# A two-layer decoder trunk on one core: every on-chip array placed at a multiple of 64 bytes

## The chip, the cores and the metric

The program runs on one core of one Trainium2 chip, in one launch. The metric is the device time of that launch in microseconds (us), the median of several executions. A core has TensorE for matrix products (its rows in a profile are PE, and PEld for the loading of the stationary operand), VectorE (DVE), ScalarE (ACT), GpSimd (POOL) and SyncE (SP), which here only issues DMA transfers. On-chip memory for operands has 128 partitions; an array takes the same byte range in each partition, so an array's place is one byte address.

## What is computed

The reference runs 256 tokens of width 2048 through two layers, all in float32. Every sub-layer has the same frame (`c` is one vector per sequence; `silu(c) @ ada_w` gives a shift, a scale and a gate per sub-layer):

```python
h = rmsnorm(x, m_pre) * (1.0 + sc_m) + sh_m
x = x + gt_m * rmsnorm(mixer(h), m_post)
h = rmsnorm(x, f_pre) * (1.0 + sc_f) + sh_f
x = x + gt_f * rmsnorm((silu(h @ wg) * (h @ wu)) @ wd, f_post)
```

The mixer of layer 0 is a diagonal state space (S5) beside a gated delta rule, that of layer 1 a gated linear attention (GLA). The feed-forward part has 5632 hidden features. Nearly all the work lies in products of 256 tokens with weights that are read once from memory, some 600 MB of them.

## The kernel before

**The big products.** A float32 product is made of three products in the format float32r: the weight w is split exactly into wh + wl, the activation h into hh + hl, and `mm3` (L219) adds hh\*wh (L222), hh\*wl (L223) and hl\*wh (L224) into the same PSUM tile. `wload` (L193) fetches a weight tile of 512 KB into `w` (L216, issued by SyncE), and `split` (L144) turns it into `wh` by a copy on ScalarE (L147) and into `wl` by a subtraction on VectorE (L148).

**Two kinds of product.** `gemm_tok` (L226) has tokens on the output's partitions: the activation (128 x 128) is stationary, and 512 columns of `wh` or `wl` are the moving operand. The feed-forward parts, the output projections and the value and gate projections of the mixers are of this kind. `gemm_feat` (L254) has features on the output's partitions: there 128 x 128 of `wh` or `wl` is stationary, and 256 columns of the activation move. A profile row names the moving operand first: `mm<-wh,hhi` moves the weight, `mm<-hhi,wh` moves the activation.

**The storage.** Four pools lie one behind the other in each partition: `cst` (constants), `ring` (six slots for `w`, three for `wh`, three for `wl`, 4096 bytes each), `sm` (small arrays, made by the helper `small`, L72) and `blk` (32 blocks of 4096 bytes, for activations and everything large). The last 12 k-chunks of weights at the ends of an output projection and the starts of the next product are *held*: they are split into blocks of `blk` instead of ring slots (L200 to L201), under the names `hwh` and `hwl`, so that all products of the first 128 tokens can run before those of the second 128. Activations that are operands of the big products (`hhi`, `hlo`, `ahi`, `alo`, `yhi` and so on) always lie in `blk`.

An allocator places the arrays in the order in which their pools were opened, and rounds each array's size up to 32 bytes. Addresses of the built program before:

```
array                     address   remainder by 64   by 128
ident (cst, first)          16512          0              0
sel (cst, 4 bytes)          19072          0              0
vcols (cst, behind sel)     19104         32             32
w  (ring, first slot)       22880         32             96
wh (ring, first slot)       47456         32             96
wl (ring, first slot)       59744         32             96
acc (sm, 4096 bytes)        72032         32             96
first block of blk          96320          0             64
end of blk                 227392
```

All ring slots have the same remainders as the first, since a slot has 4096 bytes, and so have all blocks of `blk`.

**The order of the work.** The weight tiles come in the order in which the products are written. Between them, `tick` (L164) emits steps of other streams: the conditioning (`ada`, L283: one tile of `ada_w` per step, summed by VectorE at L321), S5's tables and scan, and the delta rule's solve. The splits are moved up in the order, so that the next tiles are split while TensorE works on the one before. `wh` and `wl` have three slots each, so ScalarE's copy of a tile waits until TensorE has used up the slot.

Of the kernel before, what the change touches and what calls it, by code (L numbers as in the profile page):

```python
"""Two conditioned decoder layers (S5 + gated DeltaNet + SwiGLU, then GLA + SwiGLU) on one core.

Products with the big weights run as float32r passes over exact splits: w = wh + wl and h = hh + hl,
where each part fits float32r, and hh*wh + hh*wl + hl*wh carries float32's accuracy.
Arrays live on chip as lists of [128, 1024] float32 blocks of one shared pool.
"""
# [6 lines left out]
F32 = mybir.dt.float32  # L13
# [9 lines left out]
P = 128  # L23
# [4 lines left out]
# Order of the program:  # L28
# how far splits of weights move up while the start, the mixer's products and its end are emitted
BOOST = (100, 30, 100)  # L30
# steps of a stream per weight tile: S5's tables, the conditioning by sub-layer, S5's scan, the delta rule's solve
# [4 lines left out]
# streams that VectorE takes up behind the latest split of weights  # L36
BEHIND = ("prep", "solve")
# which of the conditioning's first parts TensorE sums
# [3 lines left out]
class Net:  # L42
# [21 lines left out]
    def pin(s, ins):  # L64
        """Keeps an instruction without operands from taking its storage long before its time."""
        return s.tc.keep_in_program_order(ins)

# [10 lines left out]
    def small(s, shape, dt=F32, tag=None, bufs=2):  # L78
        return s.sm.tile(shape, dt, tag=tag or "s" + "_".join(map(str, shape)), name="small", bufs=bufs)

# [1 line left out]
    def consts(s):  # L82
# [14 lines left out]
        # rows 0, 32, 64 and 96 are one  # L97
        s.sel = s.cst.tile([P, 1], F32, name="sel")
        nc.vector.tensor_reduce(out=s.sel, in_=s.ident[:, 0::32], axis=AX.X, op=ALU.add)

    def picks(s):
        nc = s.nc
        # pick[:, j, 32:64] picks every fourth token from j on, with zeros to both sides
        z = s.b(name="pick0")[:, :384].rearrange("p (j n) -> p j n", j=4)
        nc.gpsimd.memset(z, 0.0)
        for j in range(4):
            nc.gpsimd.tensor_copy(z[:, j, 32:64], s.ident[:, j::4])
        s.pick = s.cst.tile([P, 4, 96], F32R, name="pick")
        nc.scalar.copy(s.pick, z)

# [1 line left out]
    def rsqrt(s, out, x, scale, eps, add=None):  # L112
        """out = (x*scale + eps)^-0.5 for small operands, to float32's accuracy; (x + add)^-0.5 * scale with add."""
        nc = s.nc
        shape = [x.shape[0], int(x.free_size())]
        if shape == [P, 1]:
            # w = -x/2, then y = y * (y * y * w + 1.5), from a seed by the bits of w
# [26 lines left out]
    def split(s, hi, lo, x):  # L144
        """hi + lo = x exactly, both in float32r."""
# [8 lines left out]
    def step(s, name):  # L154
        """Emits one step of a stream; False at its end."""
# [28 lines left out]
    def finish(s, name):  # L184
        while s.step(name):
            pass
# [7 lines left out]
    def wload(s, ap, a, b, hold=False):  # L194
        """A tile of weights [128, a, b] on chip and split: [(hi, lo)] along a."""
# [23 lines left out]
    def mm3(s, ps, lhs, rhs, st, en):  # L219
        """ps (+)= lhs^T rhs over split operands."""  # L220
# [5 lines left out]
    def gemm_tok(s, W, n0, nw, kcs, lhs, ps=None, st=True, en=True, hold=0, late=False):  # L226
        """[256 tokens, nw] = h @ W[:, n0:n0+nw] over k-chunks kcs, one PSUM tile per 128 tokens.
        The last `hold` k-chunks of weights stay on chip for the second 128 tokens, which then run behind
        the first (after all of theirs, if late)."""
# [3 lines left out]
        per = 4  # L233
# [20 lines left out]
    def gemm_feat(s, W, n0, kcs, lhs, nw=256):  # L254
        """[nw features, 256 tokens] = (h @ W[:, n0:n0+nw])^T, one PSUM tile per 128 features."""
# [14 lines left out]
    def vectors(s):  # L270
        """Vectors over features as columns: V[name] is [128, chunks]."""
# [19 lines left out]
    def row_sums(s, ps, wv, k, first, last):  # L291
        """ps[32j + any, :] (+)= silu(c)_k^T W_k for the four k-chunks k + j, side by side in the array's columns."""
# [4 lines left out]
    def ada(s, layer, sec, finish, pe=False):  # L297
        """Generator: one of the six parts of silu(c) @ W + B, by halves; finish(q, sums, e) gets a quarter's partial
        sums, still to be added over the partitions that e selects. The products run on VectorE, or on TensorE."""
# [84 lines left out]
    def squares(s, x, out):  # L384
        """out = the sums of squares of [128, n <= 512] x."""
# [3 lines left out]
    def rstd(s, x, out):  # L389
        """1 / rms of one token tile [128, 2048] in two halves."""  # L390
# [12 lines left out]
    def pre(s, x, t, S, H, hi, lo):  # L403
        """h^T = ((x / rms(x)) * S + H)^T of token tile t, split, into the blocks of k-chunks hi and lo.
        1 / rms goes in with the transposing product (first tile, shortest chain) or before it (least of TensorE)."""
# [39 lines left out]
    def out_part(s, W, kcs, lhs, y):  # L445
        """Adds h @ W over some k-chunks to y, or makes y where there is none."""
# [14 lines left out]
    def post(s, W, kcs, lhs, y, x, G, then, hold):  # L461
        """x + G * rms-normed (y + h @ W), in place of x; then(t) follows for each token tile."""
# [34 lines left out]
    def transposed(s, src, hi, lo, t, deep=None):  # L497
        """Four [128 tokens, 128] pieces of src into a block of k-chunks, split."""
# [45 lines left out]
    def gla(s, h, x, G, then):  # L544
# [3 lines left out]
        # gate logits: low-rank, tokens first, then by features  # L548
# [53 lines left out]
        # q and k by features, scaled by their decays  # L602
# [29 lines left out]
        # attention weights, keys on partitions: [tile 0 own, tile 1 own, tile 0 for queries of tile 1]  # L632
# [28 lines left out]
        # v, and the heads' outputs  # L661
# [31 lines left out]
    def gla_mm(s, ps, f, items):  # L693
        """Products over the two feature chunks of a head: the first chunk's sums are kept on chip by PSUM."""
# [9 lines left out]
    def s5_load(s):  # L704
        """b and c, two groups of a state on the partitions."""
# [9 lines left out]
    def s5_prep(s):  # L715
# [37 lines left out]
        # sin and cos of th, reduced to [-pi, pi]  # L753
# [50 lines left out]
        # columns: state on partitions, tiles along the free axis  # L804
# [17 lines left out]
        # e^(i*4*theta*c), c < 64  # L822
        s.s5_cos = [s.b(name="s5cos") for _ in range(2)]
        s.s5_sin = [s.b(name="s5sin") for _ in range(2)]
        for hf in range(2):
# [10 lines left out]
            while m < 64:  # L836
# [3 lines left out]
                # e^(i*m) from e^(i*m/2), squared  # L840
# [16 lines left out]
        # b and c with the state on partitions: [128, 32 tiles, 16]  # L857
# [24 lines left out]
        # d on the diagonal of the first lag  # L882
# [16 lines left out]
        for ig in range(4):  # L899
# [44 lines left out]
            # lags 0..3 of the groups' kernels  # L944
# [25 lines left out]
    def s5_run(s, pu, out):  # L970
        """Generator: u (PSUM, tokens on partitions, 512 channels a half) to the split y by features, in out."""
# [8 lines left out]
        for hf in range(2):  # L980
            yT, hi, lo = None, None, None
            for qq in range(2):
                ig = hf * 2 + qq
                # chunks of 4 tokens on the partitions, picked by columns of the identity
# [40 lines left out]
                # states before each chunk  # L1025
# [12 lines left out]
                # outputs: [64 chunks, (j, p)] per group  # L1038
# [49 lines left out]
    def gdn_masks(s):  # L1088
        nc = s.nc
        # level l: rows in the lower half of block b of 2^(l+1), columns (b, 2^l)  # L1090
# [9 lines left out]
    def gdn_conv(s, ps, fc, out, cw):  # L1100
        """silu of the causal convolution of one feature chunk [128, 256], out of PSUM."""
# [6 lines left out]
    def gdn_gates(s, ps):  # L1108
        """beta and the running sums of g from the projections a, b (tokens on partitions)."""
# [18 lines left out]
        # softplus(z) = max(z, 0) + log1p(e), the latter with what 1 + e rounds off  # L1128
# [442 lines left out]
```

## Time and profile before

| | us |
|---|---|
| median of three executions | 2604.7 |
| the three executions | 2600.22, 2604.7, 2609.11 |
| span of the profiled execution, first to last instruction | 2602.8 |
| PE busy, share of the span | 2508.7, 96% |
| DVE busy | 1733.1, 67% |
| ACT busy | 1108.0, 43% |

The profile is of one execution, of which it gives the span alone; the span is 1.9 us under the median, and the three executions lie 8.9 us apart. In a row of a group, `xN` is the number of instructions, and behind it stand their busy time together and the mean of one. "Min/median/max" rows give durations in nanoseconds. Products overlap in TensorE, so one lasts longer than the time from its start to the start of the next; what a stretch of products costs is read from starts. PEclk is the clock that was granted to TensorE as a share of the full one. The profile shows these stages: up to 165 us the first conditioning and `u`, to 607 us the mixer of layer 0, 659 to 1403 us its feed-forward part, 1410 to 1829 us GLA, 1865 to 2593 us the last feed-forward part.

### The profile page before, as it was taken

The page shows a single profiled execution, that of the slowest core. Times are in us where ns is not written, and L with a number is a line of the kernel's source. Part 1 is how long each engine was busy: PE and PEld are TensorE (multiplying, and loading weights), DVE is VectorE, ACT ScalarE, POOL GpSimd, SP SyncE. Part 2 cuts the span into 40 slices and gives each one's busy share as a digit, 9 for nine tenths or more (in the row PEclk, how much of TensorE's full clock was granted, in tenths as well). Part 3 has the DMA queues.
Part 4 walks back from the last instruction along what each step waited for, and adds up shares of the span by engine and source line. Part 5 has one row for each costly group of instructions (what it writes and reads, how often), then busy time and mean ns, then how long its engine had stood idle before and what let it go on. Part 6 is the DMA issues. An engine that isn't in the chain of part 4 may idle for free.

```text
span 2602.8 us, 34554 instructions
## 1 busy us (share of the span) xinstructions
PE 2508.7 (96%) x13142; PEld 2028.4 (78%) x13142; DVE 1733.1 (67%) x2294; ACT 1108.0 (43%) x1416; POOL 84.8 (3%) x135
## 2 busy tenths in 40 slices
PE   5999999987999999999998999999999999999998
PEld 2577889865777888887786897787788788888886
DVE  6866797678677676777778677676655544444446
ACT  3354553435334444433445533444544444433443
POOL 1120001000000000000000000000000000000000
PEclk9999999998999999999999999999999999999999
DMA  8877567576788888988886586788466565556554
GB/s 277 318 246 251 171 208 249 179 261 235 237 299 289 293 289 286 314 305 303 292 283 213 159 272 222 244 292 275 150 209 210 190 187 186 181 184 191 184 182 137
DMA packets 298983, 615.15 MB, mean 236 GB/s; under 512 B 24368, under 2 KB 61680, under 8 KB 298816
## 3 DMA queue, kind: packets, MB, share of 16 engines
q1 hardware_dynamic: 294240, 604.32, 70.0%
q0 software_dynamic: 2304, 4.93, 0.6%
q10 hardware_dynamic: 2272, 3.68, 0.4%
q8 instruction: 103, 1.69, 0.3%
q14 instruction: 64, 0.52, 0.1%
HBM read 610.10 MB, written 2.10 MB: 235 GB/s over the span
## 4 chain that ended last, share of the span: by engine, by line
PE 84%; DVE 6%; DMA 5%; ACT 3%; issue 2%; SPq 0%; ACTq 0%; DVEq 0%; POOL 0%
PE mm L223 25%; PE mm L222 24%; PE mm L224 24%; DMA w<-in_ada_w_dram 4%; PE tp L295 2%; DVE wl L148 1%; DVE small L321 1%; PE tp L503 1%; PE tp L331 1%; ACT small L428 1%; DMA w<-in_w_out_dram 1%; ACT small L387 1%; PE tp L1247 1%; PE tp L1253 1%; PE tp L1006 1%
## 5 line engine op out<-in xcount | busy, mean ns | idle before, releaser
L148 DVE TENSOR_TENSOR wl<-w,wh 128x1024 fp32r<-128x1024 f32 x722 | 878.7, 1222 | 559.2 <-ACT wh L147 557.6
L147 ACT CAST wh<-w 128x1024 fp32r<-128x1024 f32 x722 | 755.4, 1047 | 1131.7 <-PE mm L224 960.5
L222 PE MATMUL mm<-wh,hhi 128*128 128x512 f32 x1720 | 685.4, 399 | 7.4 <-DVE hhi L433 4.5
L223 PE MATMUL mm<-wl,hhi 128*128 128x512 f32 x1720 | 684.1, 398 | 6.5 <-DVE wl L148 6.4
L224 PE MATMUL mm<-wh,hlo 128*128 128x512 f32 x1720 | 682.1, 397 | 0.7 <-DVE hlo L434 0.7
L321 DVE SCALAR_TENSOR_TENSOR small<-w,silu_c,small 128x1024 f32<-128x1024 f32 x288 | 370.4, 1286 | 135.9 <-DMA w<-in_ada_w_dram 128.7
L223 PEld LDWEIGHTS mm<-wl,hhi 128*128 128x128 f32 x1720 | 324.1, 188 | 87.8 <-DVE wl L148 9.6
L222 PEld LDWEIGHTS mm<-wh,hhi 128*128 128x128 f32 x1720 | 323.1, 188 | 86.6 <-DVE hhi L433 5.2
L224 PEld LDWEIGHTS mm<-wh,hlo 128*128 128x128 f32 x1720 | 324.0, 188 | 80.6 <-DVE hlo L434 1.7
L222 PE MATMUL mm<-wh,ahi 128*128 128x512 f32 x656 | 260.5, 397 | 0.0
L224 PE MATMUL mm<-wh,alo 128*128 128x512 f32 x656 | 259.1, 395 | 0.0
L223 PE MATMUL mm<-wl,ahi 128*128 128x512 f32 x656 | 259.1, 395 | 0.0
L224 PE MATMUL mm<-hhi,wl 128*128 128x256 f32 (+1 forms) x544 | 154.0, 283 | 2.4 <-DVE wl L148 2.4
L222 PE MATMUL mm<-hhi,wh 128*128 128x256 f32 (+1 forms) x544 | 155.5, 286 | 0.1
L223 PE MATMUL mm<-hlo,wh 128*128 128x256 f32 (+1 forms) x544 | 153.8, 283 | 0.0
L223 PEld LDWEIGHTS mm<-wl,ahi 128*128 128x128 f32 x656 | 123.0, 188 | 30.3 <-issue 0.5
L222 PEld LDWEIGHTS mm<-wh,ahi 128*128 128x128 f32 x656 | 123.0, 187 | 30.1 <-ACT wh L147 0.5
L224 PEld LDWEIGHTS mm<-wh,alo 128*128 128x128 f32 x656 | 122.9, 187 | 30.1
L224 PEld LDWEIGHTS mm<-hhi,wl 128*128 128x128 f32 (+1 forms) x544 | 100.1, 184 | 4.4 <-DVE wl L148 2.6
L222 PEld LDWEIGHTS mm<-hhi,wh 128*128 128x128 f32 (+1 forms) x544 | 100.2, 184 | 3.4 <-issue 1.5
L223 PEld LDWEIGHTS mm<-hlo,wh 128*128 128x128 f32 (+1 forms) x544 | 100.3, 184 | 1.1 <-issue 0.3
L295 PE MATMUL tp<-w,silu_c 128*32 128x512 f32 x384 | 67.4, 632 | 10.3 <-DMA w<-in_ada_w_dram 5.7
(430 smaller groups left out, 2463.8 us busy)
## 6 DMA issues: line engine op xcount, KB each, us to landing
w<-in_ada_w_dram SPq DMA_DIRECT2D x384, 512.0 KB, 5.3
w<-in_ffn_gate_dram SPq DMA_DIRECT2D x176, 512.0 KB, 4.5
w<-in_ffn_up_dram SPq DMA_DIRECT2D x176, 512.0 KB, 4.5
w<-in_ffn_down_dram SPq DMA_DIRECT2D x176, 512.0 KB, 4.8
w<-in_w_in_dram SPq DMA_DIRECT2D x160, 512.0 KB, 5.1
w<-in_w_out_dram SPq DMA_DIRECT2D x64, 512.0 KB, 5.3
w<-in_s_glu_w_dram SPq DMA_DIRECT2D x8, 512.0 KB, 4.9
x<-in_x_dram SPq DMA_DIRECT2D x4, 512.0 KB, 6.0
```

What stands on the lines that cost most here:

```text
L147: s.nc.scalar.copy(hi, x)
L148: s.subs.append(s.nc.vector.tensor_tensor(out=lo, in0=x, in1=hi, op=ALU.subtract).ins)
L222: mm(ps, lhsT=lhs[0], rhs=rhs[0], start=st, stop=False)
L223: mm(ps, lhsT=lhs[0], rhs=rhs[1], start=False, stop=False)
L224: mm(ps, lhsT=lhs[1], rhs=rhs[0], start=False, stop=en)
L295: s.nc.tensor.matmul(ps[32 * j : 32 * j + 32, :], lhsT=lhsT, rhs=w, start=first, stop=last)
L321: nc.vector.scalar_tensor_tensor(out=acc, in0=wv[:, 0], scalar=s.sc[:, g : g + 1], in1=acc, op0=ALU.mult, op1=ALU.add)
L331: s.nc.tensor.matmul(ps[:, m : m + 1], lhsT=acc[:, m * P : m * P + P], rhs=e[:, 0:1], start=True, stop=True)
L387: s.nc.scalar.activation(out=dump[:, : int(x.free_size())], in_=x, func=AF.Square, accum_out=out)
L428: nc.scalar.activation(out=hf[:, js], in_=ps[:, js], func=AF.Identity, scale=S[:, k : k + 1], bias=H[:, k : k + 1])
L503: nc.tensor.transpose(ps[:, js], src[:, js], s.ident)
L1006: nc.tensor.matmul(pp[:, i * 64 : i * 64 + 64], lhsT=s.s5_win[ig][e][:, i * P : i * P + P], rhs=us[:, i * 64 : i * 64 + 64], start=True, s ...
```

## The change

Arrays in `cst` and `sm` are made as large as the next multiple of 64 bytes, and a view of the size asked for is handed out. `sel`, the one array of `cst` with less than 64 bytes, is widened in the same way. Since all later addresses follow from these sizes, every array from `vcols` on moves:

```
array                     before    after   remainder by 64   by 128
vcols (cst)                19104    19136         0             64
w  (ring, first slot)      22880    22912         0              0
wh (ring, first slot)      47456    47488         0              0
wl (ring, first slot)      59744    59776         0              0
acc (sm)                   72032    72064         0              0
first block of blk         96320    97600         0             64
end of blk                227392   228672
```

The blocks of `blk` move by 1280 bytes, from one multiple of 64 to another. Engine by engine, the instructions, their operands, their waits and their order are the same in both programs; only the addresses in them differ (and the line numbers of the source).

```diff
+LINE = 16
...
     def small(s, shape, dt=F32, tag=None, bufs=2):
-        return s.sm.tile(shape, dt, tag=tag or "s" + "_".join(map(str, shape)), name="small", bufs=bufs)
+        tag = tag or "s" + "_".join(map(str, shape))
+        n = math.prod(shape[1:])
+        line = LINE if dt == F32 else 2 * LINE
+        if shape[0] != P or n % line == 0:
+            return s.sm.tile(shape, dt, tag=tag, name="small", bufs=bufs)
+        t = s.sm.tile([P, -(-n // line) * line], dt, tag=tag, name="small", bufs=bufs)[:, :n]
+        if len(shape) == 2:
+            return t
+        names = "abcd"[: len(shape) - 1]
+        return t.rearrange(f"p ({' '.join(names)}) -> p {' '.join(names)}", **dict(zip(names, shape[1:])))
...
-        s.sel = s.cst.tile([P, 1], F32, name="sel")
+        s.sel = s.cst.tile([P, LINE], F32, name="sel")[:, 0:1]
```

## The prediction

> **What bounds the kernel now.** I read the page's busy line and its chain first.
>
> ```profile
> PE 2508.7 (96%) x13142; PEld 2028.4 (78%) x13142; DVE 1733.1 (67%) x2294; ACT 1108.0 (43%) x1416; POOL 84.8 (3%) x135
> PE 84%; DVE 6%; DMA 5%; ACT 3%; issue 2%; SPq 0%; ACTq 0%; DVEq 0%; POOL 0%
> PE mm L223 25%; PE mm L222 24%; PE mm L224 24%; DMA w<-in_ada_w_dram 4%; PE tp L295 2%; DVE wl L148 1%; DVE small L321 1%; PE tp L503 1%; PE tp L331 1%; ACT small L428 1%; DMA w<-in_w_out_dram 1%; ACT small L387 1%; PE tp L1247 1%; PE tp L1253 1%; PE tp L1006 1%
> ```
>
> TensorE is busy for 96% of the span, and the three products of the split multiplication are 73% of the chain that ended last. Whether the supply of weights could be the hidden bound is read from the groups by line: what did the engines that split wait for?
>
> ```profile
> L147 ACT CAST wh<-w 128x1024 fp32r<-128x1024 f32 x722 | 755.4, 1047 | 1131.7 <-PE mm L224 960.5 <-PE mm L223 88.4 <-DMA w<-in_w_in_dram 42.7
> L148 DVE TENSOR_TENSOR wl<-w,wh 128x1024 fp32r<-128x1024 f32 x722 | 878.7, 1222 | 559.2 <-ACT wh L147 557.6
> L148 DVE TENSOR_TENSOR hwl<-w,hwh 128x1024 fp32r<-128x1024 f32 x40 | 48.1, 1220 | 4.9 <-ACT hwh L147 4.9
> L147 ACT CAST hwh<-w 128x1024 fp32r<-128x1024 f32 x40 | 40.7, 1055 | 11.1 <-DMA w<-in_ffn_down_dram 5.7 <-DMA w<-in_w_out_dram 5.3
> ```
>
> ScalarE's copy into a ring slot sat idle for 1131.7 us, of which 1048.9 until a product had given the slot back, and 42.7 for a DMA. The splits run ahead of TensorE; TensorE is the bound, so the time of one product counts.
>
> **The change part by part.** Nothing is added or removed; addresses change. Of the operands of the big products only those in the ring get another remainder by 64 (32 becomes 0); all in blk are at 0 before and after. So the question is what a product pays for a moving operand at remainder 32, and the kernel holds its own comparison: held weights lie in blk, at remainder 0. The next view is that of single tiles: durations in ns (least, median, most), first of ring weights, then of held ones.
>
> ```profile
> L222 PE MATMUL mm<-wh,hhi x1720: 388/396/798, 52.3 to 2524.0; 128*128 128x512 f32 x192
> L222 PE MATMUL mm<-wh,ahi x656: 393/396/792, 824.4 to 2575.3; 128*128 128x512 f32 x164
> L222 PE MATMUL mm<-wh,yhi x104: 393/396/792, 1736.9 to 1811.6; 128*128 128x512 f32 x104
> L222 PE MATMUL mm<-wh,yahi x64: 393/396/632, 474.7 to 548.8; 128*128 128x512 f32 x64
> L222 PE MATMUL mm<-wh,ybhi x48: 388/396/628, 549.5 to 594.6; 128*128 128x512 f32 x48
> ```
>
> ```profile
> L222 PE MATMUL mm<-hwh,hhi x72: 387/389/632, 632.7 to 1864.2; 128*128 128x512 f32 x72
> L222 PE MATMUL mm<-hwh,ahi x48: 389/389/395, 1386.9 to 2591.7; 128*128 128x512 f32 x48
> L222 PE MATMUL mm<-hwh,yhi x24: 389/389/395, 1812.3 to 1828.0; 128*128 128x512 f32 x24
> ```
>
> The same form has a median of 396 ns from the ring and 389 from blk, in each stage. Products overlap, so the cost is taken from starts. The timeline of TensorE around the end of the first feed-forward part has the ring's last products and, right behind them, the held ones:
>
> ```profile
> 1376.37 0.39 PE L222 MATMUL mm<-wh,ahi 128*128 128x512 f32 x1
> ...
> 1386.87 0.39 PE L222 MATMUL mm<-hwh,ahi 128*128 128x512 f32 x1
> ...
> 1388.25 0.39 PE L222 MATMUL mm<-hwh,ahi 128*128 128x512 f32 x1
> ...
> 1402.53 0.39 PE L222 MATMUL mm<-hwh,ahi 128*128 128x512 f32 x1
> ```
>
> From 1376.37 on, 45 ring products start in the 10.50 us up to the first held one at 1386.87: 233.3 ns each. From 1388.25 to 1402.53 start 63 held ones in 14.28 us: 226.7 ns each. The first six held ones (1386.87 to 1388.25, 1.38 us) took 230, a short run-in. The difference is 6.6 ns per product, which at 512 columns in 226.7 ns is the time of about 15 columns. A run of 64 bytes is 16 float32 columns, so one more such run per product would fit an operand that begins in the middle of one; that is my reading, and no row shows it.
>
> Is it the address, or something else about the held products? They run for one token tile at a time, where the ring's alternate. But the ring also has such a run, where a feed-forward part starts with the first token tile alone:
>
> ```profile
> 628.89 0.40 PE L222 MATMUL mm<-wh,hhi 128*128 128x512 f32 x1
> ...
> 630.76 0.39 PE L224 MATMUL mm<-wh,hlo 128*128 128x512 f32 x1
> ```
>
> Eight starts in 1.87 us are 233.8 ns each: the ring's time, in the held order. Nor is it less traffic. Here are a stretch of held products and the last feed-forward part (the columns are busy us and instructions of PE, PEld, DVE, ACT and POOL, then the granted clock, the DMA share and GB/s):
>
> ```profile
> 1812.00:1828.00 16.00, 16.00 (x72) 13.20 (x72) 11.23 (x22) 7.01 (x14) 0.00 (x0) 1.00 0.70 248
> 1865.00:2576.00 711.00, 711.00 (x3093) 571.94 (x3091) 356.66 (x326) 293.63 (x312) 0.00 (x0) 1.00 0.60 189
> ```
>
> The held stretch has more DMA (0.70 against 0.60) and more VectorE work (70% against 50%), and its products are the shorter ones. What is left is where the moving operand lies.
>
> *The sum.* The five groups of L222 have 1720 + 656 + 104 + 64 + 48 = 2592 products, and mm3 issues three of each: 7776 products with a moving operand of 512 columns in the ring. At 6.6 ns that is 51.3 us at most. How much arrives at the end depends on the stage. Three stretches with their products that read wh (two in three of them):
>
> ```profile
> 659.00:1386.00 727.00, 632.55 (x1996) 1.00 0.85 292
> 1565.00:1812.00 247.00, 208.24 (x655) 1.00 0.77 254
> 1865.00:2576.00 711.00, 631.10 (x1999) 1.00 0.60 189
> ```
>
> and all engines in the two of them not yet shown, then in two early stretches:
>
> ```profile
> 659.00:1386.00 727.00, 724.49 (x3179) 581.78 (x3178) 526.40 (x483) 293.14 (x311) 14.64 (x21) 1.00 0.85 292
> 1565.00:1812.00 247.00, 246.67 (x1071) 195.19 (x1070) 175.50 (x224) 108.27 (x133) 4.89 (x7) 1.00 0.77 254
> 52.00:165.00 113.00, 104.05 (x801) 68.09 (x801) 94.16 (x217) 44.02 (x65) 19.02 (x20) 0.97 0.84 294
> 475.00:607.00 132.00, 121.05 (x671) 97.84 (x671) 103.69 (x174) 52.12 (x77) 2.93 (x4) 0.96 0.72 249
> ```
>
> In the three steady stretches TensorE is idle for 2.5, 0.3 and 0.0 us, so each ns of a product is a ns of the span: (1996 + 655 + 1999) x 3/2 = 6975 products, 46.0 us. I take off 2 us for run-ins: transposes break up the products, and if three breaks in 192 products each cost six products 3.3 ns, that is 0.3 ns on each. The other 801 products (5.3 us) lie where TensorE is idle for some 8% of the time; I count half, 2.6, since some of a shorter product then turns into waiting. Together 46.0 - 2.0 + 2.6 = 46.6 us.
>
> *The other operands.* With weights stationary (gemm_feat) the moving operand is in blk already. Loading the stationary one took
>
> ```profile
> L222 PEld LDWEIGHTS mm<-wh,hhi 128*128 128x128 f32 x1720 | 323.1, 188 | 86.6 <-DVE hhi L433 5.2 <-ACT wh L147 4.5 <-issue 0.5
> L222 PEld LDWEIGHTS mm<-hhi,wh 128*128 128x128 f32 x512 | 97.2, 190 | 2.8 <-issue 1.5 <-ACT qkv L1106 0.8
> ```
>
> 188 ns from blk and 190 from the ring. Loads run beside the product before, so I take 0; the far end is 2 ns for the 3 x 512 = 1536 such products of this form, 3.1 us of gain. Splits: into blk they took 1220 and 1055 ns, into the ring 1222 and 1047, so between 2 ns less and 8 ns more; ScalarE's thousand us of waiting for TensorE cover either, and without that cover 8 ns x 722 would be 6 us. DMA into the ring: I take 0. Transfers of 512 KB land in a median of 5.3 us in the ring and 6.0 (x) in blk, so nothing speaks for a faster landing at remainder 0; and L147 hardly waits for them (42.7 us above).
>
> ```profile
> w<-in_ada_w_dram SPq DMA_DIRECT2D x384, 512.0 KB, 5.3
> x<-in_x_dram SPq DMA_DIRECT2D x4, 512.0 KB, 6.0
> ```
>
> The span of 2602.8 would become 2556.2; with the 1.9 us between span and median, 2604.7 - 46.6 = 2558.
>
> **The rivals.**
>
> *No effect.* The address is not what makes held products short; something in how they stand in the program is, such as their short, late runs. For it: the three rows count only 144 held products of L222, and their run-in of 230 ns is not explained by an address. Against it: the rows at 628 us, and the same 389 ns in every stage. Time 2604.7. In the Trainium skill, the page "SBUF — State Buffer", section "Specifications (TRN2)", says that on-chip lines have 16 bytes. By that, an operand at remainder 32 already begins on a line and 2048 bytes touch 128 lines either way, so the change would do nothing and the time would stay at 2604.7; the 396 and 389 ns speak against that.
>
> *Supply becomes the bound in the first feed-forward part.* There the DMA share is 0.85 with 292 GB/s; 2.8% shorter products ask for 300 GB/s. If the transfers couldn't follow, its 1996 x 3/2 x 6.6 ns = 19.8 us would turn into waits of L147 for DMA: 2604.7 - 26.8 = 2578. Against it: that copy waits for TensorE today.
>
> *Slower: the throttle takes it back and more.* Denser products could be granted less clock. TensorE holds 84% of the chain, 2186 us, so 1% of clock costs 22 us; the granted mean is
>
> ```profile
> core 0: 2602.8 us, clock 0.988
> ```
>
> and the gain is gone at 2.1% less (0.967). At 0.95 the time would be 2558 + 2186 x (0.988/0.95 - 1) = 2645. Against it: the clock reads 1.00 in the three steady stretches, and also at 1812 to 1828 us, where products already start 227 ns apart.
>
> **How the numbers follow.** My forecast has 80%, no effect 9%, supply 7%, throttle 4%. The first and third are faster: 0.87 faster, 0.09 within 0.3% (7.8 us, about what a measurement of this kernel can tell from no change), 0.04 slower. The range reaches down to all 51.3 us and the 3.1 of stationary operands (2550.3) with some scatter of the executions, 2548, and up to the supply case, 2578.
>
> **What would show it.** In the profile after: ring products at a median of 389 ns where they have 396, starts about 227 ns apart in the last feed-forward part; PE still without idle time there; L147 still waiting for PE; L147, L148 and the held products unchanged; the span shorter by some 20 us in each feed-forward part and 6 in GLA. Ring products at 396 would prove my reading of the address wrong; 389 with new idle time before L222 and L223 would be the supply case; a clock below 0.97 the throttle.

## The result, and the profile after

The changed kernel takes 2569.9 us (median of four executions, 2565.23 to 2577.51) against 2606.9 us for the kernel before on the same chip: a ratio of 0.9867, with a 95% interval of 0.9845 to 0.9889. The profiled execution took 2569.16 us with a span of 2567.5, so the span became 35.3 us shorter and the median 37.0 us, where 46.6 was forecast. Lines from L28 on have other numbers now: L222, L223 and L224 are L234, L235 and L236; the splits L147 and L148 are L159 and L160.

The view of single tiles of the changed kernel (durations in ns, then first and last start) answers to the rows of 396 and 389 ns:

```profile
L234 PE MATMUL mm<-wh,hhi x1720: 387/394/798, 51.8 to 2489.6; 128*128 128x512 f32 x192
...
L234 PE MATMUL mm<-wh,ahi x656: 388/388/794, 815.1 to 2539.9; 128*128 128x512 f32 x164
...
L234 PE MATMUL mm<-wh,yhi x104: 388/392/794, 1714.3 to 1789.5; 128*128 128x512 f32 x104
...
L234 PE MATMUL mm<-wh,yahi x64: 387/392/502, 475.4 to 545.5; 128*128 128x512 f32 x64
```

```profile
L234 PE MATMUL mm<-hwh,hhi x72: 387/389/628, 629.8 to 1842.0; 128*128 128x512 f32 x72
...
L234 PE MATMUL mm<-hwh,ahi x48: 389/389/398, 1367.5 to 2556.3; 128*128 128x512 f32 x48
...
L234 PE MATMUL mm<-hwh,yhi x24: 389/389/391, 1790.2 to 1805.8; 128*128 128x512 f32 x24
```

The held products stayed at 389 ns. Those of the ring came down from 396 to values between 388 and 394, and not every row moved alike. Starts are the better measure. The timeline of TensorE at the end of the first feed-forward part, where the prediction read 233.3 and 226.7 ns:

```profile
1357.22 0.39 PE L234 MATMUL mm<-wh,ahi 128*128 128x512 f32 x1
...
1367.53 0.40 PE L234 MATMUL mm<-hwh,ahi 128*128 128x512 f32 x1
...
1368.91 0.40 PE L234 MATMUL mm<-hwh,ahi 128*128 128x512 f32 x1
...
1383.21 0.39 PE L234 MATMUL mm<-hwh,ahi 128*128 128x512 f32 x1
```

45 ring products in the 10.31 us up to 1367.53 are 229.1 ns each; 63 held ones from 1368.91 to 1383.21 are 227.0. So the ring's products are 4.2 ns cheaper, not 6.6, and still cost 2 ns more than held ones. Where the 35.3 us arose can be read from first and last starts in the rows of tiles, here and in the prediction:

| | before | after | gain so far |
|---|---|---|---|
| first `wh,yahi` (S5's output projection) | 474.7 | 475.4 | -0.7 |
| first `hwh,hhi` (feed-forward part begins) | 632.7 | 629.8 | 2.9 |
| first `wh,ahi` | 824.4 | 815.1 | 9.3 |
| first `hwh,ahi` (its end) | 1386.9 | 1367.5 | 19.4 |
| first `wh,yhi` (GLA's output projection) | 1736.9 | 1714.3 | 22.6 |
| first `hwh,yhi` (its end) | 1812.3 | 1790.2 | 22.1 |
| last `hwh,hhi` (last feed-forward part begins) | 1864.2 | 1842.0 | 22.2 |
| last `hwh,ahi` | 2591.7 | 2556.3 | 35.4 |

Two things stand out: the last feed-forward part gave 13.2 us, and GLA's output projection, with 312 ring products, gave nothing. The three steady stretches of the changed kernel, cut at the same products (busy us and instructions of PE, PEld, DVE, ACT, POOL, then granted clock, DMA share, GB/s):

```profile
1842.70:2540.60 697.90, 697.90 (x3092) 573.05 (x3091) 356.57 (x326) 294.76 (x312) 0.00 (x0) 1.00 0.64 193
655.80:1367.50 711.70, 711.70 (x3182) 583.88 (x3181) 527.61 (x484) 294.83 (x312) 14.63 (x21) 1.00 0.87 298
1545.00:1790.00 245.00, 243.41 (x1072) 195.38 (x1071) 175.44 (x224) 108.48 (x133) 4.88 (x7) 1.00 0.78 256
```

In both feed-forward parts TensorE is busy throughout, also in the first, where it was idle for 2.5 us before; in GLA it is idle for 1.6 us in 245, where it was idle for 0.3 before. What it waits for there (TensorE's waits from 1640 to 1815 us; two more in this view, of 1.5 and 0.2 us, lie behind GLA's last held product at 1806 us; before, the view had one wait of 0.3 us), and VectorE's own row of events ahead of the longest one:

```profile
PE mm L235 <- DVE wl L160: 1.0, 1, 1.0
```

```profile
1730.50 1.28 DVE L333 SCALAR_TENSOR_TENSOR small<-w,silu_c,small 128x1024 f32<-128x1024 f32 x1 [1.77 <-DMA w<-in_ada_w_dram]
1733.27 1.28 DVE L333 SCALAR_TENSOR_TENSOR small<-w,silu_c,small 128x1024 f32<-128x1024 f32 x1 [1.48 <-DMA w<-in_ada_w_dram]
1734.47 3.49 DVE L160 TENSOR_TENSOR wl<-w,wh 128x1024 fp32r<-128x1024 f32 x3
```

VectorE stands idle for 1.77 and 1.48 us until tiles of `ada_w` have landed, and three splits queue up behind these sums; at 1735 us TensorE waits for one of them. ScalarE's copy still waits mostly for TensorE:

```profile
L159 ACT CAST wh<-w 128x1024 fp32r<-128x1024 f32 x722 | 757.7, 1050 | 1102.8 <-PE mm L236 923.3
```

### The profile page after: what moved, and what is told of

Read it like the earlier page. It is cut to its first block, busy times and chain, and to the rows that moved or that the text cites. A ratio compares the mean times of both kernels' runs of the same rounds, so it can differ in the third digit from the quotient of the medians.

```text
span 2567.5 us, 34554 instructions
## 1 busy us (share of the span) xinstructions
PE 2475.1 (96%) x13142; PEld 2029.8 (79%) x13142; DVE 1734.0 (68%) x2294; ACT 1109.9 (43%) x1416; POOL 84.7 (3%) x135
## 4 chain that ended last, share of the span: by engine, by line
PE 84%; DVE 6%; DMA 5%; ACT 3%; issue 2%; ACTq 0%; SPq 0%; DVEq 0%; POOL 0%
PE mm L236 25%; PE mm L235 25%; PE mm L234 24%; DMA w<-in_ada_w_dram 3%; PE tp L307 2%; DVE small L333 1%; DVE wl L160 1%; DMA w<-in_w_in_dram 1%; PE tp L515 1%; PE tp L343 1%; ACT small L440 1%; DMA w<-in_w_out_dram 1%; ACT small L399 1%; PE tp L1259 1%; PE tp L1265 1%
## 5 line engine op out<-in xcount | busy, mean ns | idle before, releaser
L160 DVE TENSOR_TENSOR wl<-w,wh 128x1024 fp32r<-128x1024 f32 x722 | 879.2, 1223 | 532.0 <-ACT wh L159 530.3
L159 ACT CAST wh<-w 128x1024 fp32r<-128x1024 f32 x722 | 757.7, 1050 | 1102.8 <-PE mm L236 923.3
L234 PE MATMUL mm<-wh,hhi 128*128 128x512 f32 x1720 | 679.7, 396 | 7.0 <-DVE hhi L445 4.2
L235 PE MATMUL mm<-wl,hhi 128*128 128x512 f32 x1720 | 676.4, 393 | 4.3 <-DVE wl L160 4.3
L236 PE MATMUL mm<-wh,hlo 128*128 128x512 f32 x1720 | 678.4, 395 | 0.7 <-DVE hlo L446 0.7
L235 PEld LDWEIGHTS mm<-wl,hhi 128*128 128x128 f32 x1720 | 324.6, 189 | 79.0 <-DVE wl L160 6.1
L234 PEld LDWEIGHTS mm<-wh,hhi 128*128 128x128 f32 x1720 | 324.0, 189 | 76.8 <-DVE hhi L445 4.9
L236 PEld LDWEIGHTS mm<-wh,hlo 128*128 128x128 f32 x1720 | 324.8, 189 | 72.8 <-DVE hlo L446 1.7
L236 PE MATMUL mm<-wh,alo 128*128 128x512 f32 x656 | 258.1, 393 | 0.0
L234 PE MATMUL mm<-wh,ahi 128*128 128x512 f32 x656 | 257.3, 392 | 0.0
L235 PE MATMUL mm<-wl,ahi 128*128 128x512 f32 x656 | 256.3, 391 | 0.0
L236 PE MATMUL mm<-hhi,wl 128*128 128x256 f32 (+1 forms) x544 | 154.4, 284 | 2.8 <-DVE wl L160 2.8
L234 PE MATMUL mm<-hhi,wh 128*128 128x256 f32 (+1 forms) x544 | 155.5, 286 | 0.0
L235 PE MATMUL mm<-hlo,wh 128*128 128x256 f32 (+1 forms) x544 | 154.3, 284 | 0.0
L235 PEld LDWEIGHTS mm<-wl,ahi 128*128 128x128 f32 x656 | 123.2, 188 | 28.5 <-issue 0.5
L234 PEld LDWEIGHTS mm<-wh,ahi 128*128 128x128 f32 x656 | 123.2, 188 | 26.6 <-ACT wh L159 0.5
L236 PEld LDWEIGHTS mm<-wh,alo 128*128 128x128 f32 x656 | 123.3, 188 | 26.0
L236 PEld LDWEIGHTS mm<-hhi,wl 128*128 128x128 f32 (+1 forms) x544 | 101.2, 186 | 4.8 <-DVE wl L160 3.2
L234 PEld LDWEIGHTS mm<-hhi,wh 128*128 128x128 f32 (+1 forms) x544 | 101.2, 186 | 3.1 <-issue 1.2
L235 PEld LDWEIGHTS mm<-hlo,wh 128*128 128x128 f32 (+1 forms) x544 | 102.1, 188 | 1.1 <-issue 0.3
```

The lines of the kernel that those rows point to most:

```text
L159: s.nc.scalar.copy(hi, x)
L160: s.subs.append(s.nc.vector.tensor_tensor(out=lo, in0=x, in1=hi, op=ALU.subtract).ins)
L234: mm(ps, lhsT=lhs[0], rhs=rhs[0], start=st, stop=False)
L235: mm(ps, lhsT=lhs[0], rhs=rhs[1], start=False, stop=False)
L236: mm(ps, lhsT=lhs[1], rhs=rhs[0], start=False, stop=en)
```

## The experiments

All times below are medians beside runs of the kernel before on the same chip; a ratio has its 95% interval behind it. The theory under test at first was the prediction's, of *lines*: an operand that begins within 64 bytes costs more. Its rival came from the 2 ns that ring products still cost more than held ones although both lie at multiples of 64: that of *pairs*, by which the distance between the moving and the stationary operand counts. Held products have both operands in `blk`, at distance 0; ring products had 96 - 64 = 32 by 256 before and have 128 - 64 = 64 after.

### Products alone (e1_grid)

A new program holds little but one moving array, one stationary array and 36 products for each pair of offsets (it was executed once, as were the two like it further down):

```python
mo = m // 4 + (i // 3 % 2) * 512
so = st // 4 + (i % 9) * 128
nc.tensor.matmul(p[:, :w], lhsT=sta[:, so : so + P], rhs=mov[:, mo : mo + w], start=i == 0, stop=i == n - 1)
```

> Products alone: 36 of one form (128x128 stationary, 512 columns moving, float32r) for each pair of a moving address (0, 16, 32, 64, 96, 128, 192, 224 bytes past a multiple of 256) and a stationary address (0, 32, 64, 128 past one), then 72 of 256 columns for six pairs; nothing else runs, and the output isn't the reference's. Line theory (only the moving operand's remainder by 64 counts): 226.7 ns from start to start at 0, 64, 128, 192, and 233.3 at 16, 32, 96, 224, whatever the stationary address. Pair theory (how the two operands lie to each other by 128 or 256 counts too): at stationary 64 the moving address 64 takes 226.7 and 0 and 128 take 229.0, and the cheap column wanders with the stationary address. If neither address matters (something else in the program made the ring slow): one time for all pairs, within 1 ns.

The timeline of TensorE, a row for each pair (`m64s0` moves from offset 64 over a stationary operand at 0). From one row's start to the next row's are 36 products:

```profile
26.37 8.32 PE L46 MATMUL m0s0x<-mov,sta 128*128 128x512 f32 x36
34.53 8.50 PE L46 MATMUL m16s0x<-mov,sta 128*128 128x512 f32 x36
...
42.87 8.57 PE L46 MATMUL m32s0x<-mov,sta 128*128 128x512 f32 x36
51.27 8.40 PE L46 MATMUL m64s0x<-mov,sta 128*128 128x512 f32 x36
59.51 8.57 PE L46 MATMUL m96s0x<-mov,sta 128*128 128x512 f32 x36
...
101.51 8.56 PE L46 MATMUL m16s32x<-mov,sta 128*128 128x512 f32 x36
109.91 8.35 PE L46 MATMUL m32s32x<-mov,sta 128*128 128x512 f32 x36
118.09 8.57 PE L46 MATMUL m64s32x<-mov,sta 128*128 128x512 f32 x36
126.49 8.41 PE L46 MATMUL m96s32x<-mov,sta 128*128 128x512 f32 x36
134.75 8.57 PE L46 MATMUL m128s32x<-mov,sta 128*128 128x512 f32 x36
```

At 0 on 0, 36 products start in 8.16 us: 226.7 ns each. 32 on 0: 8.40 us, 233.3 ns. 64 on 0: 8.24 us, 228.9 ns. These are the three values seen in the kernels: held, ring before, ring after. And 32 on 32, where nothing lies at a multiple of 64, takes 8.18 us or 227.2 ns, while 64 on 32 takes 233.3 and 96 on 32 takes 229.4. Multiples of 64 don't decide. Among offsets at multiples of 32, where all operands of the kernel's big products lie, the difference of the two does: pairs with the same difference by 256 agree within 1 ns. Its sign counts too, since 0 on 64 took 233.3 (the row from 159.98 to 168.38 us).

### One part of the change, and the step back (e2_ring_alone, e3_ring_back, e4_ring_as_blk)

e2 is the kernel before with the ring moved, e3 the changed kernel with the ring moved on by another 32 bytes, e4 the changed kernel with the ring at the same remainder by 256 as `blk`. Some constants of `cst`, which lie ahead of the ring, move along in all three; none of them is an operand of the big products:

```diff
 e2, to the kernel before: ring at 128 by 256, blk keeps 64
-        s.sel = s.cst.tile([P, 1], F32, name="sel")
+        s.sel = s.cst.tile([P, 16], F32, name="sel")[:, 0:1]
+        s.sm.tile([P, 56], F32, tag="fill", name="fill", bufs=1)
 e3, to the changed kernel: ring at 160 by 256, blk at 64
+        s.cst.tile([P, 8], F32, name="fill")
+        s.sm.tile([P, 56], F32, tag="fill", name="fill", bufs=1)
 e4, to the changed kernel: ring and blk at 64 by 256
+        s.cst.tile([P, 48], F32, name="fill")
+        s.sm.tile([P, 16], F32, tag="fill", name="fill", bufs=1)
```

> The kernel before with the ring alone moved by 32 bytes to the address that it has after the change; the small arrays keep remainder 32, the blocks keep remainder 64 by 256. Ring theory: ring products 229.0 ns apart as after the change, 2570 us. Rival, that the small arrays bring part of it: more than 2573, up to 2605 if they bring it all.

> The changed kernel with the ring alone put back to remainder 32 by 64; small arrays and blocks stay where the change put them by 64 and 256. Ring theory: 233.3 ns, 2605 us. Rival, that the small arrays bring part of it: under 2602.

> The changed kernel with the ring moved on by 192 bytes, so that ring and blocks both lie 64 past a multiple of 256 (before: ring 96, blocks 64; after the change: ring 128, blocks 64). Pair theory: ring products as cheap as held ones, 226.7 ns instead of 229.0, so 7776 x 2.3 ns = 18 us less than the changed kernel, 2552 us. Line theory (the last 2.3 ns come from something else than the address): 229.0 ns and 2570 us.

e2: 2576.7 us, 0.9889 (0.9873 to 0.9905), ring products 229.0 ns apart as in the changed kernel. That is 28.9 us under the kernel before, where the change brought 37.0, and it lies in the range that was expected if the small arrays brought a part; but the two intervals overlap, and e3 speaks against such a part. e3: 2608.6 us, 1.0008 (0.9998 to 1.0019), 233.4 ns at a distance of 96: with the ring off again, nothing of the change is left, though everything in `sm` and `cst` still has its rounded size. e4: 2573.0 us, 0.987 (0.985 to 0.989). Its ring products start 227 ns apart, 2 ns less than in the changed kernel, and yet its time is no shorter. In the last feed-forward part, where TensorE is busy throughout, the gain is there: from the last `hwh,hhi` to the last `hwh,ahi` e4 takes 708.0 us and the changed kernel 714.3. Up to there e4 has come 9.1 us later (1851.1 against 1842.0). Products with stationary weights got dearer (119.8 ns from start to start, on the mean of starts under 130 ns, against 116.4 in the changed kernel), as their pairs did in the first program (120 ns each); the rest went elsewhere. TensorE's waits in GLA say where some of that went:

```profile
PE mm L236 <- DVE wl L161: 5.5, 4, 2.7
```

It waits 5.5 us for splits, in four waits of which the longest is 2.7, where the changed kernel waits 1.0 in this view. With faster products TensorE meets VectorE's late splits there.

### Lines against pairs in the whole kernel (e5_all_at_32, e6_apart_128)

Two kernels that set the two theories against each other. In e5 no operand of a big product lies at a multiple of 64, but the distance is 64; in e6 all of them do, but the distance is 128:

```diff
 e5, to the kernel before: ring 96 by 256, blk 32
+        s.sm.tile([P, 56], F32, tag="fill", name="fill", bufs=1)
 e6, to the changed kernel: ring 128 by 256, blk 0
+        s.sm.tile([P, 48], F32, tag="fill", name="fill", bufs=1)
```

> The kernel before, with one array of 224 bytes more in sm, so that blk begins at remainder 32 by 64 too. The ring stays where it was (96 by 256), blk goes from 64 to 32 by 256: no operand of a big product lies at a multiple of 64 bytes, and ring less blk is +64 by 256, as in the changed kernel. The theory of lines (an operand costs more when it begins within 64 bytes): ring products stay 233.3 ns apart, the held ones go up to that too, about 2608 us. The theory of pairs (what counts is the distance of the moving from the stationary operand, by 256): ring products 229.0 ns apart, held ones 226.7, products with stationary weights and 256 columns near 115, about 2571 us.

> The changed kernel, with one array of 192 bytes more in sm, so that blk begins at 0 by 256 and the ring at 128: every operand lies at a multiple of 64 bytes, as the change has it, but ring less blk is +128 and not +64. The theory of lines: nothing changes, about 2570 us. The theory of pairs: ring products 233.3 ns apart again, held ones 226.7, about 2605 us, as slow as the kernel before.

The last 45 ring products of the last feed-forward part, first in e5, then in e6 (the row of the first and of the held one behind them):

```profile
2534.69 0.39 PE L223 MATMUL mm<-wh,ahi 128*128 128x512 f32 x1
...
2544.99 0.40 PE L223 MATMUL mm<-hwh,ahi 128*128 128x512 f32 x1
```

```profile
2566.06 0.40 PE L235 MATMUL mm<-wh,ahi 128*128 128x512 f32 x1
...
2576.53 0.39 PE L235 MATMUL mm<-hwh,ahi 128*128 128x512 f32 x1
```

e5: 10.30 us, 228.9 ns each; 2574.7 us, 0.9886 (0.9871 to 0.9901). e6: 10.47 us, 232.7 ns each; 2600.6 us, 0.9986 (0.9974 to 0.9998), next to nothing. So the kernel becomes fast without one aligned operand in its big products, and stays slow with all of them aligned. The theory of lines has fallen; that of pairs stands in both.

### Which distances, and what in them (e8_grid2, e11_grid3)

> Products alone: one moving and one stationary array, no splits, no weights from memory, and an output that isn't the reference's, since all else is left out. Names tell the distance of the moving from the stationary operand in bytes and the width of the stationary one in columns (d64w128), h those of 256 moving columns. The theory of pairs: 226.7 ns apart at distances 0, 256 and 512, 228.9 at 64 and 320, 233.3 at 384 and at nearly all others. If the cause is that the loading of the next stationary operand and the reading of the moving one disturb each other, a narrower stationary operand (64 or 32 columns) loses less, and at 32 columns the distances differ by little; if the distance acts in another way, the width changes nothing. For 256 columns: 120 at 0, 118 at 64 and 128, 113 at 192.

The same program as the first, with other offsets and with narrower stationary operands (`lhsT=sta[:, so : so + lw]`). The number behind `d` is the distance in bytes, that behind `w` the columns of the stationary operand:

```profile
151.56 8.33 PE L44 MATMUL d240w128x<-mov,sta 128*128 128x512 f32 x36
159.73 8.36 PE L44 MATMUL d256w128x<-mov,sta 128*128 128x512 f32 x36
...
184.55 8.33 PE L44 MATMUL d512w128x<-mov,sta 128*128 128x512 f32 x36
192.71 8.44 PE L44 MATMUL d0w64x<-mov,sta 128*64 128x512 f32 x36
200.99 8.48 PE L44 MATMUL d32w64x<-mov,sta 128*64 128x512 f32 x36
...
225.79 8.49 PE L44 MATMUL d0w32x<-mov,sta 128*32 128x512 f32 x36
234.12 8.54 PE L44 MATMUL d32w32x<-mov,sta 128*32 128x512 f32 x36
242.50 8.51 PE L44 MATMUL d64w32x<-mov,sta 128*32 128x512 f32 x36
```

A distance of 240 takes 8.17 us or 226.9 ns a product, 512 takes 226.7. Without the first nine products of a row, 256 takes 226.7 as 0 does, 320 takes 228.9 as 64 does, and 384 takes 232.1 as 128 does: the pattern repeats after 256 bytes. For offsets between the multiples of 32 the distance by 256 doesn't settle it: 240 on 0, which is 16 short of a period, is as good as 0 on 0, but 16 on 32, at the same distance by 256, took 233.3 ns in the first program (8.40 us from 101.51). Why is open. With a stationary operand of 64 columns distance 0 takes 230.0 and distance 64 less, 228.4; with one of 32 columns 0 takes 231.4, and 32 bytes off 232.8. So a narrower load makes distances matter less, as a disturbance by the load should, but it makes the best case worse, which that idea doesn't explain.

> Products alone again (output without meaning, all else left out): does the distance to its own stationary operand count, or to the one that is loaded meanwhile for the next product? The stationary operands take turns at 0, 32 and 128 by 256; the moving one lies at the remainder of its own (own), of the next product's (next), or of the last one's (prev) stationary operand, so that the distance is 0 to that one and 32, 96, 128, 160 or 224 to the others. If only its own counts: own 226.7, next and prev 233. If the operand being loaded for the next product counts: next 226.7, own and prev 233. Neither: all near 233. Base (all at 0) 226.7 and far (32 off) 233.3 stand beside them. The same with 256 columns at distance 192: 113.3 against 118; hbase 113.3, hfar (distance 0) 120.

Here the stationary operands take turns at three remainders, and the moving one follows its own, the next or the last:

```python
mo = (off[(i + near) % 3] + shift) // 4 + (i // 3 % 2) * 512
so = off[i % 3] // 4 + (i % 9) * 128
```

```profile
25.70 8.32 PE L44 MATMUL basea<-mov,sta 128*128 128x512 f32 x36
33.86 8.57 PE L44 MATMUL fara<-mov,sta 128*128 128x512 f32 x36
42.27 8.53 PE L44 MATMUL owna<-mov,sta 128*128 128x512 f32 x36
50.63 8.41 PE L44 MATMUL nexta<-mov,sta 128*128 128x512 f32 x36
58.88 8.52 PE L44 MATMUL preva<-mov,sta 128*128 128x512 f32 x36
67.24 8.64 PE L44 MATMUL hbasea<-mov,sta 128*128 128x256 f32 x72
75.72 8.80 PE L44 MATMUL hfara<-mov,sta 128*128 128x256 f32 x72
```

Base 226.7 and far 233.6 are there again. Own takes 8.36 us or 232.2 ns, prev 232.2, and next 229.2 (these three stand twice in the run and agree within 0.3 ns): near the operand that is being loaded for the next product it is cheaper by 3 ns, but not as cheap as with all three near. Of the three the next load has most to do with it, and none accounts for all. The Trainium skill, page "TensorE: Matmul & The Clock Gate", section "Step-by-step: what each phase is for", says that loading the next weights takes no read bandwidth from the running product. These runs show at least that the one doesn't run without regard to the other: 229.2 against 232.2 ns, with nothing else changed than which of three stationary operands the moving one is near. And one expectation failed outright: 256 columns at distance 192 took 8.48 us for 72 products (hbasea), 117.8 ns each, where the run before had 113.3 for the same distance. For that form the distance is not all; what else decides was not found.

### A better version, and what is late next (e7_both_near, e9, e10, e12)

e7 puts ring and `blk` at one remainder by 256, and weights that will be stationary 64 bytes further, so that all products have a good distance:

```diff
+        s.sm.tile([P, 8], F32, tag="fill", name="fill", bufs=1)
-    def wload(s, ap, a, b, hold=False):
+    def wload(s, ap, a, b, hold=False, off=0):
-                wh = s.ring.tile([P, 1024], F32R, tag="wh", name="wh", bufs=s.WH)
+                wh = s.ring.tile([P, 1088], F32R, tag="wh", name="wh", bufs=s.WH)[:, off : off + 1024]
...
-            ws = s.wload(Wv[:, k0 : k0 + per, n0 : n0 + nw], per, nw)
+            ws = s.wload(Wv[:, k0 : k0 + per, n0 : n0 + nw], per, nw, off=16)
```

> The kernel before, with ring and blk at the same remainder by 256 (96), and each slot for wh and wl 256 bytes longer, so that weights that will be stationary can be placed 64 bytes further into it. Moving weights then lie at distance 0 from their stationary operand, and the moving activation at -64 from stationary weights. The theory of pairs: ring products 227 ns apart (7776 times 6.3 less than before is 49 us), products with stationary weights about 114 (2 us or more besides); if all of it arrived, 2605 - 51 = 2554 us. The run with ring and blk at one remainder lost about 5 us in GLA's output projection to splits of VectorE that came late and some more to half-clock windows, so 2554 to 2568. The theory of lines (operands at remainder 32): no gain over the kernel before, 2605.

2566.1 us, 0.9857 (0.9834 to 0.988). The products became what was expected, 227.0 ns apart in the ring; the sum did not arrive, 38.5 us out of 51. The waits of TensorE and VectorE's events at the longest of them:

```profile
PE mm L224 <- DVE wl L149: 4.8, 3, 2.4
```

```profile
1735.07 1.28 DVE L322 SCALAR_TENSOR_TENSOR small<-w,silu_c,small 128x1024 f32<-128x1024 f32 x1 [3.04 <-DMA w<-in_ada_w_dram]
...
1738.83 3.49 DVE L149 TENSOR_TENSOR wl<-w,wh 128x1024 fp32r<-128x1024 f32 x3
```

Part of the missing time had gone before GLA: e7 reaches S5's output projection 4.5 us later than the kernel before (479.2 against 474.7). In GLA VectorE is idle again, for 3.04 us (and 1.26 more in the row left out), until `ada_w` has landed, with three splits behind. So the next theory: the supply of `ada_w` is late, and fewer such sums during GLA would help. e9 and e12 take e7 with a lower rate (45 and 37 of these sums run between the first feed-forward part and GLA's held products, in place of 59), e10 is the kernel before with the rate of e9:

```diff
-AR = (2.2, 1.25, 1.04, 0.3)
+AR = (2.2, 1.25, 0.8, 0.3)
 e12: 0.66 in place of 0.8
```

> The version with ring and blk at one remainder (ring products 227 ns apart), and 0.8 instead of 1.04 conditioning tiles per weight tile during GLA: some 14 of its 59 sums of ada_w move from GLA into the last feed-forward part, where the DMA share is lowest. The theory: in GLA's output projection it is the supply that is late next, since VectorE's sums of ada_w wait there for their DMA (3.0 and 1.3 us at 1735 us) with splits queued behind them, and TensorE waits 2.4 us for such a split and gets a half-clock window behind it; with fewer sums these waits go, the 312 products of the projection take 70.8 us (227 ns each) instead of 78.6, and GLA is shorter by 4 to 9 us: about 2559 us in place of 2566. The rival (the waits come from the splits themselves, or the moved sums make waits in the last feed-forward part): no gain, 2566 or more.

> The control: the kernel before with the same 0.8 in place of 1.04. Its ring products are 233 ns apart and the output projection of GLA shows no wait of TensorE for a split over 0.4 us, so by the theory moving the sums brings nothing: 2604 to 2606 us, within 0.1%. If it gains some 6 us too, the sums cost time whatever the products take, and the waits are not what the faster products uncovered.

> The same as the run with 0.8, with 0.66: some 8 more sums of ada_w leave GLA (59 at first, some 47 at 0.8, some 38 now). At 0.8 the output projection of GLA took 73.4 us in place of 78.6, with one wait of 1.3 us for a split left; but of the 7.6 us between the two profiled executions 4.7 had arisen ahead of GLA, in stages that the edit doesn't touch, so it is open how much of the gain belongs to the edit. The theory (the supply of ada_w holds up the splits in GLA): the last waits shrink too, the projection takes 71 to 72 us, and the time is 2557 to 2561 us, again some 5 us under the run with 1.04. The rival (the gain at 0.8 was mostly the scatter of executions): 2563 to 2567 us, whatever the projection takes.

e9: 2559.1 us, 0.9824 (0.981 to 0.9838). e10: 2605.1 us, 1.0002 (0.9991 to 1.0013), so the rate alone brings the kernel before nothing. Its waits for splits in GLA even grew with the rate of e9, from 0.3 us to 2.3:

```profile
PE mm L223 <- DVE wl L148: 2.3, 2, 1.6
```

But e12: 2567.1 us, 0.9846 (0.983 to 0.9862), where a smaller rate should have done no worse. Its interval overlaps that of e9, so it isn't shown to be slower either. Here are TensorE's waits in e9 and in e12, then VectorE's events in e12:

```profile
PE mm L224 <- DVE wl L149: 2.7, 3, 1.3
```

```profile
PE mm L224 <- DVE wl L149: 3.7, 2, 2.3
```

```profile
1732.44 1.28 DVE L322 SCALAR_TENSOR_TENSOR small<-w,silu_c,small 128x1024 f32<-128x1024 f32 x1 [4.48 <-DMA w<-in_ada_w_dram]
```

With the fewest sums VectorE still stands idle for 4.48 us for one tile of `ada_w`, and TensorE waits 3.7 us, against 2.7 in e9 and 4.8 in e7. The place of the wait is confirmed in all of them: a sum that waits for its tile, splits behind it. That fewer sums cure it is not: e12 missed the theory's range and came out at the upper edge of the rival's, and more than half of e9's gain over e7 may be scatter, since 4.7 of the 7.6 us between their profiled executions arose ahead of GLA. The granted clock differs as well: over GLA's output projection it was 0.98 in e7 and e12 and 1.00 in e9. Why single tiles of `ada_w` land late there stays open. What holds is that e9 is faster than both kernels of this study: its interval lies below that of the change.

## Why the prediction was right, and where its size was not

**What bounds the kernel, right.** TensorE's products are the bound, and time taken off a ring product is time taken off the span: in the last feed-forward part 2999 ring products gave 13.2 us, 4.4 ns each, with no new idle time. ScalarE's copy still waits for TensorE (923.3 of 1102.8 us), and the splits and held products kept their times.

**The address decides, right; how it decides, wrong.** The step that failed is the reading that an operand pays for beginning "in the middle" of 64 bytes, by which ring and held products would cost the same after the change. The comparison inside the kernel was sound as a measurement (233.3 against 226.7 ns) but not as a model: held products differ from ring products in the remainder of the moving operand and also in its distance from the stationary one. e5 and e6 separate the two. The rounding to 64 bytes worked because it happened to turn a distance of 32 into one of 64. That was luck: at 128, where every operand is rounded just as well, e6 gained next to nothing.

**The term that was mis-sized.** 6.6 ns per product were forecast, and about 4.3 came. On the 6975 products of the steady stretches that is 46.0 us forecast and 30 due. The 2 us taken off for run-ins were not lost in the last part (4.4 ns came, not 4.0). The first feed-forward part gave 16.3 us (728.0 to 711.7, from 658.9 and 655.8 us to the first held product at its end) where 2997 x 4.3 = 12.9 were due; two waits for splits of 0.7 and 1.6 us, at 682 and 710 us before, are gone there. GLA, from the first ring product of its values to its first held one, gave 2.1 us (247.2 to 245.1) where 984 x 4.3 = 4.2 were due: TensorE's idle time, behind the sums of `ada_w`, grew by 1.3 us (0.3 to 1.6), and 0.8 us stay open.

**The early stages** gave 2.9 us where 2.6 were forecast, but not by the forecast's working. Two stretches of both kernels (busy us and instructions of PE, then the granted clock, DMA share, GB/s), first before, then after:

```profile
165.00:345.00 180.00, 176.15 (x1566) 1.00 0.67 215
475.00:550.00 75.00, 71.77 (x462) 0.95 0.64 216
```

```profile
165.00:345.00 180.00, 175.98 (x1549) 0.97 0.66 211
475.00:550.00 75.00, 72.00 (x491) 1.00 0.67 226
```

In the first, the clock went from 1.00 to 0.97, and the 768 products with stationary weights took 169.8 us in place of 167.7. In the second it went from 0.95 to 1.00, and the 192 ring products of S5's output projection took 70.9 us in place of 75.0, where their price explains 192 x 4.3 = 0.8. The Trainium skill, page "TensorE: Matmul & The Clock Gate", section "What's actually happening", describes a gate that halves the clock in free-running windows of about 3.4 us; 0.95 of 75 us fits two of them. Where such windows fall differs from kernel to kernel here, so a few us in a stage with many waits are no evidence about an address.

**The stationary operands** were put at 0, with 2 ns for each of 1536 products as the far end, and by the starts the far end is what came: consecutive 128 x 128 products with stationary weights start 118.3 ns apart before and 116.4 after, on the mean of starts under 130 ns. The working was wrong, since these products are pairs as well, with the distance reversed (224 by 256 before, 192 after). Little of it reached the end: in layer 0 the lower clock took it back, and from the end of the first feed-forward part to GLA's output projection the gain grew by 3.2 us (19.4 to 22.6), of which 696 ring products at 4.3 ns explain 3.0.

**The rivals.** *No effect* is excluded by the interval. The 16-byte lines that the Trainium skill states (page "SBUF — State Buffer", section "Specifications (TRN2)") say nothing about the distance between two operands, and by them neither this change nor e5 would have gained. *Supply in the first feed-forward part* didn't come: DMA went from 292 to 298 GB/s there, with no idle time of TensorE. A late transfer did become a wait, but in GLA and through VectorE. *The throttle* didn't come: the mean clock went from 0.988 to 0.985, and the steady stretches stayed at 1.00.

## What to carry to other kernels

Before you align anything, measure the product alone over a few pairs of offsets: here, among multiples of 32 bytes, the distance between the moving and the stationary operand by 256 decided, worth 3% of a product with 512 columns, and the alignment of either to 64 did not. A comparison found inside a kernel gives a price only if its two sides differ in nothing but what the change will change; list what else differs, and ask which of it the change leaves. And when the bound engine gets faster, look for the work that was only just in time: the next 2 ns per product (e7) brought 38.5 us in all where 51 were due, in part because splits stood behind a sum that waited for its transfer.

## What the runs showed of the hardware

- Products of float32r with 512 columns, each with its own 128 x 128 stationary operand, start 226.7 ns apart at a distance of 0 bytes, 228.9 at 64, and 232 to 234 at the other multiples of 32, with a period of 256 bytes. At odd multiples of 16 it was 231 to 235, except 226.9 for 240 on 0; 16 on 32, the same distance by 256, took 233.3.
- With 256 moving columns the order is another: 120.0 ns at distance 0 and 113.3 or 117.8 at 192, in two runs of the same distance. In e7 both values stand side by side: of 1588 such starts two in three lie 113 or 114 ns behind the one before, most others 117 to 119.
